# Combining the second FFN matrix's quarters ahead of time, and one difference of hidden tiles in the up stage

## Chip, cores and metric

The kernel runs on one core of a Trainium2 chip. The metric is the device time of one execution in microseconds.

## The reference, cut to what matters

A backbone of two layers over 1024 latent tokens and 256 context tokens of width 1024. Layer 0 mixes tokens by neighbourhood attention and differential attention (the "even attention"), layer 1 by grouped-query attention and a Hyena convolution. Each layer ends in a gated FFN with a hidden width of 2816:

```
def conv_ffn(h, w_up, conv_w, conv_b, w_down):
    g, v = jnp.split(h @ w_up, 2, axis=-1)
    g = dwconv3(g, conv_w, conv_b)
    return (jax.nn.silu(g) * v) @ w_down
```

Here `w_up` is 1024x5632 and `w_down` 2816x1024. Layer 1 needs no context tokens after its mixer.

## The kernel before, in words

Everything is kept transposed: 128 features on the partitions, tokens along the free axis. The hidden width is 22 tiles (`NJ`) of 128 features. Products in float32 are made of three matmuls (`mm3`, lines 73 to 75): both factors are split into a rounded high part and the rest, by a ScalarE copy (`split`, line 63) and a VectorE subtraction (line 68). A weight tile of 128x512 goes through `whalf`, a hidden tile through `hsplit`.

**Up stage** (`ffn`, lines 968 to 1018). For each hidden tile `j` the products are made with Strassen-like sums, the convolution and the gate run on ScalarE and VectorE, and the hidden tile `t` goes to DRAM (`hd[j]`, line 1018).

**Down stage** (`down`). The latent tokens' product with `w_down` is again Strassen-like: `w_down` is cut in four quarters (halves of the hidden width and of the output, called 11, 12, 21, 22), the hidden tiles as well (the hidden tiles' halves by the halves of the tokens), each of 11 tiles (`H`). There are four rounds `r`, each of 11 steps `k`. Rounds 0 to 2 have two products per step, into the PSUM sets `Y` and `Z` (24 matmuls of 128x512), round 3 one (12 matmuls). What a step needs is made beforehand:

- Weights, in `down_w` (lines 885 to 924): in round 0 four quarter tiles are loaded (256 KB each) and GpSimd makes three sums of them (lines 910 to 912); in round 1 two loads and one sum (917); in round 2 two loads; in round 3 two loads and one sum (923). `wnext` keeps 6 split halves ahead.
- Hidden tiles, in `prep` (1121 to 1137): in round 0 VectorE makes two differences (1126, 1127) and two splits; in rounds 1 and 2 GpSimd makes one difference (1131, 1135). Hidden tiles are loaded back from `hd` (1095) into tiles that the up stage has used.

In layer 0 the context tokens' down product (`down_ctx`) stands between the up stage and round 0.

**Even attention** (`attn_even`, lines 549 to 561). Four differential heads (`da_head`) and four pairs of neighbourhood heads (`na_pair`) take turns. Work goes in ticks (`tick`, line 507), nine for each of them: scores on TensorE into PSUM, VectorE takes them out (654), ScalarE makes exponents (631, 673), VectorE joins the two maps of a differential head (736), TensorE transposes (487) and multiplies (529, 755) one or two ticks later. GpSimd has little to do here: it normalizes the neighbourhood maps (635, 602) and makes a reciprocal root (134) for each group of a differential head, which VectorE needs next (152). Queries come by DMA into two pairs of buffers (462).

The order of instructions on each engine is set when the program is built, by a scheduler that works from its own estimate of the timing; an engine then runs its instructions in that order, and the DMA queue of SyncE issues its transfers in order too, each after what it waits for.

Of the kernel before, what the change touches and what calls it, by code (L numbers as in the profile page):

```python
# [2 lines left out]

# [1 line left out]

# [5 lines left out]
F32 = mybir.dt.float32  # L11
# [7 lines left out]
KT = 8  # L19
NL = 1024  # L20
# [19 lines left out]
class Kernel:  # L40
# [466 lines left out]
    def tick(self):  # L507

        self.step += 1
        due = [f for n, f in self.queue if n <= self.step]  # L510
        self.queue = [x for x in self.queue if x[0] > self.step]
        for f in due:
            f()
# [35 lines left out]
    def attn_even(self, first):  # L549

        with ExitStack() as es:
            p = self.pool(es, "ev", "right")
            pp = self.pool(es, "evp", psum=True)
            self.order(p, [("mn", 16, 6), ("sm", 16, 6), ("mc", 16, 6), ("s1", 16, 2), ("rsv", 16, 4), ("rsr", 16, 4), ("yeps", 16, 2),
                           ("ptc", 512, 2), ("y0", 256, 3), ("ysq", 256, 2), ("pt", 2048, 4), ("pr", NT, 6), ("tb", NAT, 2), ("v", NT, 2),
                           ("q", 512, 2), ("k", NT, 2)])
            n = {"D": 0, "N": 0}
            for c in "DNDNDNDN":
                (self.na_pair if c == "N" else self.da_head)(p, (self.ek, p)[sum(n.values()) % 2], pp, n[c], first if n == {"D": 0, "N": 0} else None)
                n[c] += 1  # L560
            self.flush()

    def load_v(self, p, src, c):

# [319 lines left out]

    def down_w(self, l, r, k, first=None):

        nc, W = self.nc, self.a["w_down"][l]
        op = nc.gpsimd.tensor_tensor
        A, S = ALU.add, ALU.subtract

        def get(names):

            src = [W[k + NJ // 2 * (n[1] == "2")][:, 512 * (n[0] == "2"):][:, :512] for n in names]
            if first:
                res = first
            elif k % 3 < 2 and r == 0 or r == 3 and (k % 2 == 1 or k > 9):
                res = [self.r2() for _ in names]
            else:
                res = []
                while len(res) < len(names):  # L900
                    t = self.wrp.tile([128, 1024], F32, tag="raw", name="raw", bufs=self.wr)
                    res += [t[:, :512], t[:, 512:]]
            for t, s in zip(res, src):
                self.wdma = nc.sync.dma_start(t, s).ins
            if first:
                self.wfirst = self.wdma
            return res
        if r == 0:
            a11, a21, a12, a22 = get(("11", "21", "12", "22"))
            op(a22, a21, a22, op=A)  # L910
            op(a11, a22, a11, op=S)
            op(a12, a12, a11, op=S)
            return [a11, a12] if first else [self.whalf(a11), self.whalf(a12)]
        if r == 1:
            a11, a21 = get(("11", "21"))
            z = self.whalf(a11)
            op(a21, a11, a21, op=S)
            return [self.whalf(a21), z]
        if r == 2:
            a12, a22 = get(("12", "22"))  # L920
            return [self.whalf(a22), self.whalf(a12)]
        a21, a22 = get(("21", "22"))
        op(a22, a21, a22, op=A)
        return [self.whalf(a22)]

    def ffn(self, l, hs, tv, xd, hd, sd, xp, last):

# [40 lines left out]
        for j in range(NJ):  # L968
            g = p.tile([128, nt], F32, tag="g", name="g", bufs=1)
            v = p.tile([128, NL], F32, tag="v", name="v", bufs=1)  # L970
            t = p.tile([128, nt], F32, tag="t", name="t", bufs=self.tb)
            late = (late + [t])[-2:]
            g1, g2, v1, v2 = (x[:, c:c + 512] for x in (g, v) for c in (0, 512))
            if ctx:
                c = self.bank("C")
            p1 = self.r2()
            if j < len(pre):
                X = None
                nc.sync.dma_start(p1, sd[j][:, :512])
# [24 lines left out]
            tt(v1, Y, p1, op=A)  # L1004
            if ctx:
                prod(c[:, NC:], "c2", True, w)
                prod(c[:, NC:], "c1", False)
            prod(Z, "22", False)
            tt(g2, u2, Z, op=A)
            if j == NJ - 1 and not ctx:  # L1010
                down = self.down(l, xd, hd, xp, last, late)
                next(down)
            self.conv(t, g, cw[:, j, :], spans)
            nc.scalar.activation(t[:, :nt], t[:, :nt], AF.Silu)
            tt(t[:, :NL], t[:, :NL], v, op=ALU.mult)
            if ctx:
                tt(t[:, NL:], t[:, NL:], c[:, NC:], op=ALU.mult)
            nc.sync.dma_start(hd[j][:, :nt], t[:, :nt])
# [5 lines left out]
    def down_ctx(self, xd, hd, xc, sq, bcx, yb, zb, last, late):  # L1024
# [2 lines left out]
        ps = [b.tile([128, 512], F32, tag="b", name="dn", bufs=4)[:, :NC] for b in (yb, zb) for _ in range(4)]  # L1027
        order = self.down_order()
        hid = {}
        first = [self.ff.tile([128, n], F32, tag=t, name="w0", bufs=1) for t, n in (("g", NT), ("v", NL))]  # L1030
        first = [t[:, c:c + 512] for t in first for c in (0, 512)]

        def prep(i):
            if i < NJ:
# [37 lines left out]
    def down(self, l, xd, hd, xp, last, late):  # L1072
# [10 lines left out]
        mid = [x for n in ("hi1", "lo1") for x in halves(self.act.tile([128, KT, 512], F32, tag=n, name="hid"), KT)]  # L1083
        tvs = [x for n in ("thi", "tlo") for x in halves(self.tp.tile([128, 4, 512], F32, tag=n, name="hid"), 4)]
        xs = [x for k in range(KT) for x in halves(xp.tile([128, 2, 512], F32, tag=f"x{k}", name="x"), 2)]
        B = {"22": tvs[0:4] + lat[0:7], "21": lat[7:16] + [mid[15], xs[15]], "12": xs[0:4] + mid[0:7], "11": tvs[4:8] + mid[7:14]}
        t12, p1, u3 = xs[4:8], mid[7:11], mid[11:15]
        self.xt = [[tvs[m], xs[8 + m]] for m in range(KT)]
        H = NJ // 2

        def load(b, k):
# [29 lines left out]
        def prep(r, k):  # L1121

            b11, b12, b21, b22 = (B[x][k] for x in ("11", "12", "21", "22"))
            if r == 0:
                z = hsplit(b22)
                tt(b12, b12, b11, op=S)
                tt(b22, b22, b12, op=S)
                return hsplit(b22), z
            if r == 1:
# [497 lines left out]
    def body(self):  # L1627
# [18 lines left out]
        self.actc = None  # L1646
        xd = dt((KT, 128, NT), "xd")
        self.nat = dt((8, 128, NAT), "nat")
        eac, ew = ExitStack(), ExitStack()
        with ExitStack() as es:  # L1650
            hs, mm = self.start(self.es, eac, ew, es)
# [226 lines left out]
```

## Time and profile before

| | |
|---|---|
| median of 3 runs | 3209.14 us (3207.26 to 3213.04) |
| the profiled execution | 3208.64 us, of which the span of the profile 3206.9 us |
| TensorE busy | 95% of the span |
| VectorE, ScalarE, GpSimd busy | 69%, 42%, 30% |
| DMA queue of SyncE | 434.35 MB, 41.4% of 16 engines |
| granted TensorE clock, mean | 0.984 |

The profile is of one execution. A busy share is an average over stages with different limits, so the stages are looked at one by one: the even attention from 521 to 885 us, the up stages from about 1040 to 1572 and 2540 to 2961 us, the down stages from 1644 to 1896 and from 2957 to 3202 us. A time in a row is counted from the start of the span.

### The profile page before, as it was taken

The page shows a single profiled execution, that of the slowest core. Times are in us where ns is not written, and L with a number is a line of the kernel's source. Part 1 is how long each engine was busy: PE and PEld are TensorE (multiplying, and loading weights), DVE is VectorE, ACT ScalarE, POOL GpSimd, SP SyncE. Part 2 cuts the span into 40 slices and gives each one's busy share as a digit, 9 for nine tenths or more (in the row PEclk, how much of TensorE's full clock was granted, in tenths as well). Part 3 has the DMA queues.
Part 4 walks back from the last instruction along what each step waited for, and adds up shares of the span by engine and source line. Part 5 has one row for each costly group of instructions (what it writes and reads, how often), then busy time and mean ns, then how long its engine had stood idle before and what let it go on. Part 6 is the DMA issues. An engine that isn't in the chain of part 4 may idle for free. (4 is left out here: it accounts for less than half of the span.)

```text
span 3206.9 us, 43513 instructions
## 1 busy us (share of the span) xinstructions
PE 3056.6 (95%) x15764; PEld 2458.4 (77%) x15764; DVE 2224.0 (69%) x3865; ACT 1340.9 (42%) x2374; POOL 964.0 (30%) x703
## 2 busy tenths in 40 slices
PE   7999989999999899999988989899999899999799
PEld 3567767777788788888876778787778677887677
DVE  7762454777757766766679687577665877766976
ACT  4322213777735333333434452226663533433343
POOL 5530220222202422222135344012330443323662
PEclk9999999999999999999999999999999999999899
DMA  6798884443253322111584446222104332224644
GB/s 239 224 301 269 246 261 129 122 126 106 81 168 111 102 82 73 65 73 65 174 288 154 135 161 163 94 76 59 36 27 148 122 109 89 86 92 154 223 144 149
DMA packets 269815, 443.03 MB, mean 138 GB/s; under 512 B 27936, under 2 KB 160160, under 8 KB 262944
## 3 DMA queue, kind: packets, MB, share of 16 engines
q1 hardware_dynamic: 265280, 434.35, 41.4%
q10 hardware_dynamic: 4320, 5.90, 0.5%
q8 instruction: 124, 2.03, 0.3%
q14 instruction: 91, 0.75, 0.1%
HBM read 338.31 MB, written 101.84 MB: 137 GB/s over the span
## 5 line engine op out<-in xcount | busy, mean ns | idle before, releaser
L68 DVE TENSOR_TENSOR wlo<-raw,whi 128x512 fp32r<-128x512 f32 x456 | 351.6, 783 | 194.4 <-ACT whi L63 187.8
L63 ACT CAST whi<-raw 128x512 fp32r<-128x512 f32 x456 | 275.3, 619 | 458.6 <-PE u L74 75.3
L134 POOL TENSOR_TENSOR rsr<-rsv,misc 128x8 f32<-128x8 f32 (+3 forms) x87 | 114.1, 1313 | 591.1 <-DVE rsv L131 343.6
L857 POOL TENSOR_TENSOR S<-raw 128x512 f32<-128x512 f32 x88 | 142.7, 1622 | 482.9 <-DMA raw<-in_w_up 407.0
L476 PE MATMUL S<-k,q 128*128 128x512 f32 (+2 forms) x1088 | 262.4, 365 | 6.4 <-DMA q<-qs 3.0
L74 PE MATMUL dn<-hs,whi 128*128 128x512 f32 x616 | 244.2, 400 | 16.5 <-DVE hs L68 16.5
L73 PE MATMUL mm<-whi,hi 128*128 128x512 f32 (+1 forms) x624 | 241.9, 389 | 2.1 <-ACT vst L393 1.1
L73 PE MATMUL dn<-hs,whi 128*128 128x512 f32 x616 | 217.5, 405 | 26.1 <-ACT hs L63 18.8
L74 PE MATMUL mm<-wlo,hi 128*128 128x512 f32 (+1 forms) x624 | 237.2, 380 | 1.6 <-DVE wlo L68 1.6
L75 PE MATMUL dn<-hs,wlo 128*128 128x512 f32 x616 | 234.9, 396 | 3.2 <-DVE wlo L68 3.2
L75 PE MATMUL mm<-whi,lo 128*128 128x512 f32 (+1 forms) x624 | 237.1, 381 | 0.7 <-DVE lo L252 0.7
L824 DVE SCALAR_TENSOR_TENSOR t<-g,cw,t 128x1008 f32<-128x1008 f32 (+1 forms) x220 | 206.3, 970 | 44.2 <-ACT t L822 43.9
L476 PEld LDWEIGHTS S<-k,q 128*128 128x128 f32 x1088 | 167.0, 189 | 42.3 <-DVE mn L654 13.0
L487 PE MATMUL T<-ident,pr 128*128 128x128 f32 x1312 | 190.5, 276 | 6.1 <-DVE pr L736 2.3
L654 DVE CUSTOM_DVE_ANT_0 pr<-S,misc,mn 128x512 f32<-128x512 f32 x256 | 185.3, 745 | 6.1 <-PE S L476 4.4
L68 DVE TENSOR_TENSOR wlo<-S,whi 128x512 fp32r<-128x512 f32 x176 | 158.1, 916 | 42.7 <-ACT whi L63 42.6
L673 ACT ACTIVATE pr<-pr,mn 128x1280 f32<-128x1280 f32 x128 | 174.5, 1367 | 30.6 <-DVE mn L654 23.1
L487 PEld LDWEIGHTS T<-ident,pr 128*128 128x128 f32 x1312 | 151.7, 141 | 44.0 <-issue 25.4
L490 ACT COPY pt<-T 128x512 f32<-128x512 f32 (+1 forms) x256 | 131.4, 523 | 85.3 <-PE T L487 82.5
L73 PEld LDWEIGHTS dn<-hs,whi 128*128 128x128 f32 x616 | 118.4, 194 | 59.3 <-ACT hs L63 23.0
L68 DVE TENSOR_TENSOR hs<-hid,hs 128x512 fp32r<-128x512 f32 x142 | 137.1, 974 | 37.7 <-ACT hs L63 36.0
L74 PEld LDWEIGHTS dn<-hs,whi 128*128 128x128 f32 x616 | 118.5, 193 | 48.4 <-DVE hs L68 23.9
(359 smaller groups left out, 7981.6 us busy)
## 6 DMA issues: line engine op xcount, KB each, us to landing
adaw<-in_w_ada SPq DMA_DIRECT2D x48, 1024.0 KB, 6.8
raw<-in_w_up SPq DMA_DIRECT2D x88, 512.0 KB, 4.0
raw<-in_w_down SPq DMA_DIRECT2D x132, 256.0 KB, 3.1
r<-in_w_down SPq DMA_DIRECT2D x84, 256.0 KB, 5.4
q<-qs SPq DMA_DIRECT2D x160, 128.0 KB, 2.2
hid<-hd SPq DMA_DIRECT2D x78, 256.0 KB, 5.3
qs<-qsg SPq DMA_DIRECT2D x120, 128.0 KB, 3.9
hd<-t SPq DMA_DIRECT2D x22, 640.0 KB, 2.9
```

The costliest lines, as they stand in the source:

```text
L63: nc.scalar.copy(hi, src)
L68: nc.vector.tensor_tensor(lo, src, f32(hi), op=ALU.subtract)
L73: mm(ps, lhsT=lh, rhs=rh, start=first, stop=False, skip_group_check=more)
L74: mm(ps, lhsT=lh, rhs=rl, start=False, stop=False, skip_group_check=more)
L75: mm(ps, lhsT=ll, rhs=rh, start=False, stop=last, skip_group_check=more)
L476: self.nc.tensor.matmul(ps, lhsT=q[:, s, c:c + 128], rhs=k[:, k0:k0 + n], start=s == 0, stop=s == 1)
L487: nc.tensor.transpose(tp[:, s, :], p_[:, k * 128:(k + 1) * 128], self.ident)
L490: eng(pt[:, s0:s0 + sn, col:col + 128], tp[:, :sn])
L654: self.nc.vector.tensor_tensor_reduce(out=dst, in0=s, in1=bias, scale=1.0, scalar=init, op0=ALU.add, op1=ALU.min, accum_out=mn)
L673: nc.scalar.activation(pr, pr, AF.Exp, bias=m[:, 1:2], scale=-1.0, accum_out=sums[j])
L824: nc.vector.scalar_tensor_tensor(t[:, o:o + n], g[:, i:i + n], cw[:, w:w + 1], t[:, o:o + n], op0=ALU.mult, op1=ALU.add)
L857: nc.gpsimd.tensor_tensor(got[n], x, y, op=op)
```

## The change

A GpSimd job is added to the even attention (`wd_steps`): for each layer and each `k` it loads the four quarter tiles of `w_down` in three column pieces (192, 192 and 128 columns, so 66 pieces in all), makes four sums of them in place and stores all four in a new DRAM tensor `ws`. Two buffers of 768 columns hold the pieces. `tick` takes two steps of this job each time (one load, one set of sums with its store). `down_w` then loads ready sums: two quarter tiles in round 0, two in rounds 1 and 2, one in round 3, and GpSimd makes no sum there. The first 11 hidden tiles have their first token half subtracted from the second in the up stage, before they are stored, so that one of the two differences of round 0 falls away. Some buffers of hidden tiles trade places.

```diff
@@ tick
         self.step += 1
+        self.beside(2)
@@ attn_even
+            self.bg = chain(self.wd_steps(0, p), self.wd_steps(1, p))
...
             self.flush()
+            self.beside(100)
@@ down_w
-        if r == 0:
-            a11, a21, a12, a22 = get(("11", "21", "12", "22"))
-            op(a22, a21, a22, op=A)
-            op(a11, a22, a11, op=S)
-            op(a12, a12, a11, op=S)
-            return [a11, a12] if first else [self.whalf(a11), self.whalf(a12)]
-        if r == 1:
-            a11, a21 = get(("11", "21"))
-            z = self.whalf(a11)
-            op(a21, a11, a21, op=S)
-            return [self.whalf(a21), z]
-        if r == 2:
-            a12, a22 = get(("12", "22"))
-            return [self.whalf(a22), self.whalf(a12)]
-        a21, a22 = get(("21", "22"))
-        op(a22, a21, a22, op=A)
-        return [self.whalf(a22)]
+        x = get((("S2", "S4"), ("11", "S3"), ("22", "12"), ("S1",))[r])
+        if first:
+            return x[:2]
+        w = [self.whalf(t) for t in x[:1 + (r < 3)]]
+        return w[::-1] if r == 1 else w
+    def wd_steps(self, l, p):
+        nc, W = self.nc, self.a["w_down"][l]
+        op = nc.gpsimd.tensor_tensor
+        A, S = ALU.add, ALU.subtract
+        for k in range(NJ // 2):
+            for c, n in ((0, 192), (192, 192), (384, 128)):
+                t = p.tile([128, 4, 192], F32, tag="wd", name="wd", bufs=2)[:, :, :n]
+                for i in range(2):
+                    nc.sync.dma_start(t[:, 2 * i:2 * i + 2], W[k + NJ // 2 * i].rearrange("p (h c) -> p h c", h=2)[:, :, c:c + n])
+                yield
+                a11, a21, a12, a22 = (t[:, i] for i in range(4))
+                op(a22, a21, a22, op=A)
+                op(a21, a11, a21, op=S)
+                op(a11, a22, a11, op=S)
+                op(a12, a12, a11, op=S)
+                nc.sync.dma_start(self.ws[l][k][:, :, c:c + n], t)
+                yield
@@ ffn, before the hidden tile is stored
+            if j < NJ // 2:
+                tt(t[:, 512:NL], t[:, 512:NL], t[:, :512], op=ALU.subtract)
@@ down, prep, round 0
                 z = hsplit(b22)
-                tt(b12, b12, b11, op=S)
                 tt(b22, b22, b12, op=S)
```

**Order on GpSimd, even attention.** Lines of the changed kernel are shifted: 134 is 135 there, 635 is 639, 602 is 606, 1131 is 1149, 857 is 861. Before, from the end of a pair of neighbourhood heads into the next differential head, GpSimd has:

```order
L602 TENSOR_SCALAR pr<-pr,sm 128x256 x4
L635 TENSOR_SCALAR pr<-pr,sm 128x640 x6
L635 TENSOR_SCALAR pr<-pr,sm 128x512 x2
L134 TENSOR_TENSOR rsr<-rsv,misc 128x2 x3
L635 TENSOR_SCALAR pr<-pr,sm 128x512 x2
```

In the change, inside a differential head (`wd` is the piece being summed):

```order
L926 TENSOR_TENSOR wd<-wd 128x192
L927 TENSOR_TENSOR wd<-wd 128x192
L135 TENSOR_TENSOR rsr<-rsv,misc 128x2
L928 TENSOR_TENSOR wd<-wd 128x192
L929 TENSOR_TENSOR wd<-wd 128x192
L926 TENSOR_TENSOR wd<-wd 128x192
L927 TENSOR_TENSOR wd<-wd 128x192
L928 TENSOR_TENSOR wd<-wd 128x192
L929 TENSOR_TENSOR wd<-wd 128x192
L135 TENSOR_TENSOR rsr<-rsv,misc 128x2
```

The reciprocal roots `rsr` that followed each other directly now stand behind or among sums of a piece.

**Order on SyncE's queue, even attention.** Before, queries follow queries (here with a head's values `v`):

```order
L462 DMA q_5060<-qs0_80 128x256 x2
L462 DMA q_5063<-qs0_80 128x256 x2
L462 DMA q_5286<-qs1_81 128x256 x2
L462 DMA q_5289<-qs1_81 128x256 x2
L462 DMA q_5173<-qs1_81 128x256 x2
```

In the change, a store of a piece (`ws0<-wd`) and the load of a later one into the same buffer stand between them:

```order
L923 DMA wd_6183<-in_w_down 128x2x192 x2
L930 DMA ws0_88<-wd_6120 512x1x128
L463 DMA q_6415<-qs0_80 128x256 x2
L570 DMA v_6536<-vsb_85 128x10x128
L923 DMA wd_6257<-in_w_down 128x2x192 x2
L930 DMA ws0_88<-wd_6183 512x1x192
L463 DMA q_6670<-qs1_81 128x256 x2
L923 DMA wd_6315<-in_w_down 128x2x128 x2
```

So a query's load is issued only after a store whose sums are done, and after a load whose buffer is free.

**Order on GpSimd, start of layer 1's down stage.** Before, behind the last sums of the up stage (`S`), triples of line 910 to 912 follow, 11 in all; the first of those shown:

```order
L910 TENSOR_TENSOR r<-r 128x512
L911 TENSOR_TENSOR r<-r 128x512
L912 TENSOR_TENSOR r<-r 128x512
L910 TENSOR_TENSOR r<-r 128x512
L911 TENSOR_TENSOR r<-r 128x512
L912 TENSOR_TENSOR r<-r 128x512
```

In the change the next after the up stage's sums is round 1's difference of hidden tiles:

```order
L861 TENSOR_TENSOR S<-raw,S 128x512
L1149 TENSOR_TENSOR hid<-hid 128x512 x2
L1149 TENSOR_TENSOR hid<-x,hid 128x512 x2
L1149 TENSOR_TENSOR hid<-hid 128x512 x7
```

In round 0 GpSimd has nothing left.

## Rows read from the trace of the kernel before

**Rows 1.** The page's first part: busy time of each engine, its share of the span, and its instructions.

```profile
PE 3056.6 (95%) x15764; PEld 2458.4 (77%) x15764; DVE 2224.0 (69%) x3865; ACT 1340.9 (42%) x2374; POOL 964.0 (30%) x703
```

**Rows 2.** Six stretches of the run, in us from the span's start: the whole even attention, one differential head, one pair of neighbourhood heads, the up stage of layer 0, the up stage of layer 1, and the start of layer 1's down stage. The columns are the stretch's length, the busy time of each engine with its instructions in brackets, the granted TensorE clock as a share of full speed, the mean busy share of the 16 DMA engines, and GB/s.

```profile
521.00:885.00 364.00, 352.79 (x2218) 284.92 (x2217) 284.69 (x964) 262.22 (x567) 71.73 (x100) 1.00 0.36 109
625.00:675.00 50.00, 48.11 (x284) 42.05 (x284) 42.63 (x137) 37.40 (x79) 7.42 (x10) 1.00 0.35 106
675.00:712.00 37.00, 36.70 (x254) 27.03 (x254) 26.25 (x99) 25.41 (x59) 10.19 (x15) 1.00 0.43 129
1100.00:1500.00 400.00, 400.00 (x2119) 345.42 (x2118) 275.69 (x350) 139.62 (x211) 100.51 (x64) 1.00 0.20 73
2720.00:2920.00 200.00, 200.00 (x884) 165.62 (x883) 141.92 (x188) 77.74 (x120) 59.26 (x40) 1.00 0.24 86
2960.00:3000.00 40.00, 21.09 (x64) 15.30 (x63) 37.73 (x29) 10.47 (x17) 33.41 (x21) 0.70 0.94 332
```

**Rows 3.** The same view, for the instructions alone that write or read the down stage's PSUM tiles `dn`: the four rounds of layer 0, then the four of layer 1. A round has 264 matmuls, the last 132; some counts are a few over, since a stretch's edge can cut a neighbour.

```profile
1644.00:1726.00 82.00, 68.20 (x264) 50.87 (x264) 1.70 (x5) 2.12 (x4) 0.94 0.71 237
1726.00:1792.00 66.00, 62.45 (x263) 49.81 (x264) 2.99 (x5) 1.12 (x3) 0.97 0.39 128
1792.00:1858.00 66.00, 61.89 (x267) 49.23 (x265) 4.82 (x8) 1.12 (x2) 1.00 0.44 141
1858.00:1896.00 38.00, 32.40 (x132) 25.61 (x132) 3.14 (x6) 0.00 (x0) 0.96 0.53 172
2957.00:3047.00 90.00, 67.36 (x264) 53.01 (x265) 0.00 (x0) 2.16 (x4) 0.87 0.70 240
3047.00:3109.00 62.00, 60.61 (x267) 49.53 (x266) 3.45 (x6) 1.63 (x3) 1.00 0.47 160
3109.00:3172.00 63.00, 60.83 (x265) 49.06 (x264) 2.80 (x5) 0.68 (x2) 1.00 0.45 146
3172.00:3202.00 30.00, 30.00 (x134) 24.75 (x132) 8.75 (x13) 0.00 (x0) 1.00 0.31 117
```

**Rows 4.** Waits of TensorE in the first round of layer 1: who waited for whom, us in total, times, longest.

```profile
PE dn L73 <- ACT hs L63: 13.7, 3, 8.7
PE dn L74 <- DVE hs L68: 6.2, 3, 3.0
```

**Rows 5.** VectorE in order of time at the start of that round (start, duration, line, operation; a bracket would give the idle time before it).

```profile
...
2970.25 1.75 DVE L68 TENSOR_TENSOR hs<-hid,hs 128x512 fp32r<-128x512 f32 x1
2971.92 2.27 DVE L824 SCALAR_TENSOR_TENSOR t<-g,cw,t 128x1008 f32<-128x1008 f32 x1
...
2988.82 2.29 DVE L1015 TENSOR_TENSOR t<-t,v 128x1024 f32<-128x1024 f32 x1
```

**Rows 6.** ScalarE in order of time there; the bracket is its idle time before, and what ended it.

```profile
...
2986.10 1.06 ACT L1014 ACTIVATE t<-t 128x1024 f32<-128x1024 f32 x1 [14.01 <-DVE t L824]
2987.06 0.60 ACT L63 CAST hs<-hid 128x512 fp32r<-128x512 f32 x1
```

**Rows 7.** Instructions of one line or tile: durations in ns as least/median/most, then the first and last start. Two of VectorE in the down stage, both inputs in SBUF; one of VectorE in the up stage, one input in PSUM; one of GpSimd in the down stage, and two of GpSimd elsewhere, for their sizes.

```profile
L68 DVE TENSOR_TENSOR hs<-hid,hs x142: 674/685/1784, 1577.5 to 3189.4; 128x512 fp32r<-128x512 f32 x142
L1126 DVE TENSOR_TENSOR hid<-hid x14: 679/1655/1787, 1645.7 to 3024.5; 128x512 f32<-128x512 f32 x14
L992 DVE TENSOR_TENSOR r<-Y,r x44: 675/681/692, 1063.1 to 2944.3; 128x512 f32<-128x512 f32 x44
L911 POOL TENSOR_TENSOR r<-r x15: 1588/1622/2122, 1645.8 to 3003.3; 128x512 f32<-128x512 f32 x15
L360 POOL TENSOR_TENSOR qz<-qy,gqack x8: 458/478/975, 1909.1 to 1939.1; 128x128 f32<-128x128 f32 x8
L857 POOL TENSOR_TENSOR S<-raw x88: 1281/1307/6639, 1023.1 to 2925.3; 128x512 f32<-128x512 f32 x88
```

**Rows 8.** VectorE in the even attention, its groups of instructions: line, operation, out<-in, shapes, count | busy us, mean ns of one | idle time before.

```profile
L654 DVE CUSTOM_DVE_ANT_0 pr<-S,misc,mn 128x512 f32<-128x512 f32 x128 | 92.4, 744 | 3.3 <-PE S L476 2.3
L736 DVE SCALAR_TENSOR_TENSOR pr<-pr,sm 128x1280 f32<-128x1280 f32 (+1 forms) x40 | 53.3, 1332 | 0.2
L152 DVE TENSOR_TENSOR dg<-ident,rsr 128x256 f32<-128x256 f32 x20 | 8.4, 421 | 3.7 <-POOL rsr L134 3.7
```

**Rows 9.** Waits in the even attention, of the DMA queue of SyncE and of VectorE: us in total, times, longest.

```profile
SPq L462 <- PE S L476: 148.8, 40, 9.8
DVE dg L152 <- POOL rsr L134: 3.7, 7, 0.6
```

**Rows 10.** DMA issues: out<-in, engine, operation, count, KB each, median us from issue to landing.

```profile
r<-in_w_down SPq DMA_DIRECT2D x84, 256.0 KB, 5.4
xd<-x SPq DMA_DIRECT2D x40, 256.0 KB, 2.3
raw<-in_w_up SPq DMA_DIRECT2D x18, 256.0 KB, 2.6
natab<-in_na_tab SPq DMA_DIRECT2D x8, 448.0 KB, 4.9
nat<-natab SPq DMA_DIRECT2D x8, 448.0 KB, 3.3
```

**Rows 11.** SyncE's queue in order of time: the same load of two successive periods (a differential head and a pair of neighbourhood heads), two periods apart.

```profile
623.28 0.37 SPq L566 DMA_DIRECT2D v<-vsa  x1
...
802.62 0.37 SPq L566 DMA_DIRECT2D v<-vsa  x1
```

More of the change, by code (lines that the diff above doesn't have):

```diff
@@ L2 @@
 from contextlib import ExitStack, nullcontext
+from itertools import chain
 import numpy as np
@@ L554, in attn_even @@
             self.order(p, [("mn", 16, 6), ("sm", 16, 6), ("mc", 16, 6), ("s1", 16, 2), ("rsv", 16, 4), ("rsr", 16, 4), ("yeps", 16, 2),
-                           ("ptc", 512, 2), ("y0", 256, 3), ("ysq", 256, 2), ("pt", 2048, 4), ("pr", NT, 6), ("tb", NAT, 2), ("v", NT, 2),
+                           ("ptc", 512, 2), ("y0", 256, 3), ("ysq", 256, 2), ("pt", 2048, 4), ("pr", NT, 6), ("tb", NAT, 2), ("v", NT, 2), ("wd", 768, 2),
                            ("q", 512, 2), ("k", NT, 2)])
+            self.bg = chain(self.wd_steps(0, p), self.wd_steps(1, p))
             n = {"D": 0, "N": 0}
@@ L885, in down_w @@
     def down_w(self, l, r, k, first=None):
-        nc, W = self.nc, self.a["w_down"][l]
-        op = nc.gpsimd.tensor_tensor
-        A, S = ALU.add, ALU.subtract
+        nc, W, ws = self.nc, self.a["w_down"][l], self.ws[l]
         def get(names):
-            src = [W[k + NJ // 2 * (n[1] == "2")][:, 512 * (n[0] == "2"):][:, :512] for n in names]
+            src = [ws[k][:, "S2 S3 S4 S1".split().index(n)] if n[0] == "S" else W[k + NJ // 2 * (n[1] == "2")][:, 512 * (n[0] == "2"):][:, :512] for n in names]
             if first:
@@ L898, in get @@
             else:
[L899 to L902, printed above, removed]
+                t = self.wrp.tile([128, 1024], F32, tag="raw", name="raw", bufs=self.wr)
+                res = [t[:, :512], t[:, 512:]]
             for t, s in zip(res, src):
@@ L907, in get, with beside @@
             return res
-        if r == 0:
-            a11, a21, a12, a22 = get(("11", "21", "12", "22"))
-            op(a22, a21, a22, op=A)
-            op(a11, a22, a11, op=S)
-            op(a12, a12, a11, op=S)
-            return [a11, a12] if first else [self.whalf(a11), self.whalf(a12)]
-        if r == 1:
-            a11, a21 = get(("11", "21"))
-            z = self.whalf(a11)
-            op(a21, a11, a21, op=S)
-            return [self.whalf(a21), z]
-        if r == 2:
-            a12, a22 = get(("12", "22"))
-            return [self.whalf(a22), self.whalf(a12)]
-        a21, a22 = get(("21", "22"))
-        op(a22, a21, a22, op=A)
-        return [self.whalf(a22)]
+        x = get((("S2", "S4"), ("11", "S3"), ("22", "12"), ("S1",))[r])
[20 more added lines that the diff above has]
+                yield
+    def beside(self, n):
+        while n and self.bg:
+            n -= 1
+            if next(self.bg, 1):
+                self.bg = None
+    bg = None
     def ffn(self, l, hs, tv, xd, hd, sd, xp, last):
@@ L1029, in down_ctx @@
         hid = {}
-        first = [self.ff.tile([128, n], F32, tag=t, name="w0", bufs=1) for t, n in (("g", NT), ("v", NL))]
-        first = [t[:, c:c + 512] for t in first for c in (0, 512)]
+        first = self.ff.tile([128, NT], F32, tag="g", name="w0", bufs=1)
+        first = [first[:, c:c + 512] for c in (0, 512)]
         def prep(i):
@@ L1085, in down @@
         xs = [x for k in range(KT) for x in halves(xp.tile([128, 2, 512], F32, tag=f"x{k}", name="x"), 2)]
-        B = {"22": tvs[0:4] + lat[0:7], "21": lat[7:16] + [mid[15], xs[15]], "12": xs[0:4] + mid[0:7], "11": tvs[4:8] + mid[7:14]}
+        B = {"22": tvs[0:2] + xs[1::-1] + lat[0:7], "21": lat[7:16] + [mid[15], xs[15]], "12": tvs[3:1:-1] + xs[2:4] + mid[0:7], "11": tvs[4:8] + mid[7:14]}
         t12, p1, u3 = xs[4:8], mid[7:11], mid[11:15]
-        self.xt = [[tvs[m], xs[8 + m]] for m in range(KT)]
+        self.xt = [[xs[3 - m] if m in (2, 3) else tvs[m], xs[8 + m]] for m in range(KT)]
         H = NJ // 2
@@ L1648, in body @@
         self.nat = dt((8, 128, NAT), "nat")
+        self.ws = [dt((NJ // 2, 128, 4, 512), f"ws{l}") for l in range(2)]
         eac, ew = ExitStack(), ExitStack()
```

## The prediction

> **What bounds the kernel now.** I read the page first: TensorE is busy 95% of the span [rows 1], so time can come only from stretches where it idles or is throttled, or be lost where it now runs. The table of stretches comes next [rows 2]. In both up stages TensorE has no idle time (400 us of 400, 200 of 200), and 884 matmuls of 128x512 in 200 us put one at 0.226 us. Then the down stages, by round [rows 3]: a round of 264 matmuls needs 264 x 0.226 = 59.7 us, the last of 132 needs 29.9. Against that the eight stretches last 82, 66, 66 and 38 us in layer 0, and 90, 62, 63 and 30 in layer 1. Lost are 22.3, 6.3, 6.3 and 8.1, then 30.3, 2.3, 3.3 and 0.1 us: 79 us, of which 52.6 in the two rounds 0. This includes the throttle: the clock of rounds 0 is 0.94 and 0.87 on average, 1.00 in most others, so parts of them ran at 1.2 instead of 2.4 GHz, after idling.
>
> Why does round 0 idle? At the start of layer 1's, TensorE waits for the hidden tiles' splits, 13.7 us for the ScalarE half and 6.2 for the VectorE half [rows 4]. In that stretch VectorE is busy 37.7 us of 40, GpSimd 33.4, and the DMA engines 94% at 332 GB/s [rows 2]. VectorE's work isn't much, it is slow: a split of 128x512 takes 0.685 us in the middle of the distribution and up to 1.78, and the difference of line 1126 has 1.655 as its median [rows 7]. The timeline shows 1.75 us for a split and 2.27 and 2.29 for the convolution and gate of the last up tile [rows 5]. ScalarE is kept in its order by that: it waits 14.0 us for the convolution (824) before its activation, and only then makes the split that TensorE wants [rows 6]. An operation of VectorE with one input in PSUM stays at 0.68 to 0.69 us in all 44 cases of the up stage, where GpSimd sums as well [rows 7]. So it is VectorE operations with both inputs in SBUF that wait for a running sum of GpSimd, by up to 1.78 - 0.68 = 1.1 us each.
>
> **Down stage: the gain.** Round 0 loses all three sums of GpSimd per step, half of the weight loads (512 KB instead of 1 MB) and one of the two differences on VectorE. Per step two weight tiles and three hidden tiles of 256 KB remain instead of four and three, 1.31 MB instead of 1.84 MB. At 24 x 0.226 = 5.4 us a step that is 243 GB/s, where the full engines gave 332 [rows 2]: not a bound any more, whereas 1.84 MB need 5.5 us, which was one. VectorE has two weight splits, two hidden splits and one difference, 5 x 0.68 = 3.4 us of 5.4, with no GpSimd operation to wait for. What is left is close to what round 1 has today (a little GpSimd work, loads at 39 to 47% of the engines), and that loses 6.3 and 2.3 us [rows 3]. Layer 0 keeps besides the entry from the context part; I put its round 0 at 9 us lost instead of 22.3. In layer 1 the stretch holds 14 matmuls of the up stage too (278 in all, 3.2 us), and VectorE has the last tile's convolution and gate to make before it can catch up, some 5 us; I put it at 10 lost instead of 30.3. Bounds: nothing gained, and 6.3 and 5.5 lost (round 1's loss, with the 3.2). Gain 13.3 + 20.3 = 33.6, between 0 and 41.
>
> Rounds 1 and 3 lose one GpSimd sum a step and round 3 half of its loads; of the 26 us lost in the six later rounds I take 5 back, between 0 and 10, since GpSimd's difference of hidden tiles stays and the waits at the rounds' ends are for PSUM and for the next norm. Gain of the down stages: 39 us.
>
> **Up stage: nothing.** 22 differences of 0.68 us (up to 1.78) go to VectorE, which is busy 276 of 400 us in layer 0 and 142 of 200 in layer 1 while TensorE has no idle time [rows 2]. The cover is the tile buffers: the gate isn't on TensorE's way until the down stage, and the last tile has no such difference. If the cover were gone it would be 22 x 1.1 = 24 us.
>
> **Even attention: the cost.** 66 pieces come in, each with two loads, four sums and a store.
>
> GpSimd: a sum of 128 columns takes 0.46 us at least, of 512 columns 1.28 [rows 7]; by a straight line 192 columns take 0.60 (an estimate). A `k` takes 8 x 0.60 + 4 x 0.46 = 6.6 us, 22 of them 146 us. A period of two heads is 18 ticks and lasts (802.62 - 623.28)/2 = 89.7 us [rows 11], 4.98 us a tick, so 66 ticks are 329 us, in which GpSimd would be busy 45% with sums, beside the 72 us of 364 that it has [rows 2]. There is room.
>
> DMA: 22 x 2.1 MB (read and written) = 46 MB in 329 us, 140 GB/s on top of 109 GB/s at a share of 0.36 [rows 2]; at the same share per byte the engines reach 0.82. Room again.
>
> VectorE: the bulk of its work there, line 654, reads scores from PSUM [rows 8], a form that rows 7 show free of waits. The 40 joins of line 736 and the 20 of line 152 have both inputs in SBUF. With GpSimd at a sum 45% of the time and half of 0.60 us left on average, each waits 0.13 us: 8 us. The 20 reciprocal roots (134) stand behind or among the sums, and VectorE waits for each root already in 7 cases, 3.7 us [rows 9]; one sum ahead makes 20 x 0.6 = 12 us. All 60 lie in differential heads, where VectorE is busy 42.6 of 50 us [rows 2], so most of it shows: 15 of the 20 us. Bounds: 0, if VectorE's idle time takes it all, and the two rivals below.
>
> SyncE's queue: a buffer's turn is load, sums, store. A load of 256 KB lands in 2.6 us, a store in 2.3 [rows 10]; with the second issue of the load, 2.2 us of sums on average, a store of up to 384 KB at some 2.6 and the hand-overs it is 8.2 us, 4.1 per piece with two buffers. That is under the 4.98 of a tick. **The Trainium skill**, "SBUF — State Buffer", section "The DMA setup-cost knee", states about 2 us fixed plus the bytes at 436 GB/s. For a piece that makes 2.9 us each way, an estimate, and about the same turn; rows 10 show 5.4 us for 256 KB in the crowded down stage, which that formula doesn't cover, so the measured rows go into the rival. Queries' loads wait in this queue anyway, 148.8 us in 40 waits for their buffers [rows 9], and with two pairs of buffers a load is issued about two ticks before its use, so a few us behind a store cost nothing as long as the chain keeps pace.
>
> **Sum.** The profiled execution took 3208.6 us. Minus 39, plus 15: 3184.6. The median of the runs is 0.5 above the profiled one, so **3185 us**.
>
> **Rivals.**
>
> *The attention hides it all.* VectorE idles 7.4 us per differential head and TensorE's waits there are short, so the 15 us may vanish, and round 0 may come down to round 1's loss with up to 5 us more. For it: the rows of the PSUM form. Against it: the differential heads' VectorE at 85%. Time 3209 - 44 = 3165 us, chance 0.26.
>
> *Only half of the gain.* If round 0 was held by the loads and the last tile's convolution rather than by GpSimd, its loss falls by half, 17 us, with 3 elsewhere. For it: the DMA engines at 94%; against it: they lose 29% of the bytes as well. Time 3209 - 20 + 15 = 3204 us, chance 0.11.
>
> *The pieces set the pace.* SyncE's queue is in order: a piece's load waits for the store two pieces back, and queries wait behind. The nearest chain of this kind under load is the mask tables': 4.9 us to load 448 KB, 3.3 to store [rows 10]. With sums of 1.62/1.28 their length [rows 7], 2.8 us, 0.4 for the second issue and 0.3 for hand-overs, a turn is 11.7 us, 5.85 per piece: 66 x (5.85 - 4.98) = 57 us, less the two ticks of slack, 10. With the 15 on VectorE it comes to 3209 - 39 + 62 = 3232 us, slower. It decides from (39 - 15 + 10)/66 = 0.5 us over the tick, a piece in 5.5 us. Chance 0.10.
>
> *VectorE pays in full in the differential heads.* Each of the 60 operations waits a whole sum of its size, 1.1 x 0.60/1.28 = 0.52 us, 31 us, and each reciprocal root half a piece, 1.2 us x 20 = 24. Time 3209 - 39 + 55 = 3225 us, chance 0.07. This is what the Trainium skill's "SBUF — State Buffer", section "Who interferes with whom", allows at worst: an exclusive lock, where a VectorE instruction with two SBUF inputs and a GpSimd operation block each other for the whole instruction. By that rule, rows 5 and 7 agree on the lock; how often the two meet it doesn't say.
>
> That the change doesn't do what it says is not a rival: the order shows no sum of GpSimd left in round 0.
>
> **How the numbers follow.** My forecast has 0.46. A measurement of this kernel can tell about 0.2%, 6.4 us, so "faster" ends at 3202.7 and "slower" begins at 3215.6. Faster: 0.46 + 0.26 and a part of the half-gain case, 0.73. Same: 0.10. Slower: the last two, 0.17. The range takes in the first rival with some of its bounds (3209 - 51 = 3158) and the half gain, and reaches to 3218, short of the two slow cases: 3158 to 3218.
>
> **What would show it.** In the profile after: GpSimd with no operation in rounds 0 and VectorE's splits there at 0.68 us; `dn` stretches of round 0 near 69 and 70 us instead of 82 and 90; the period of two heads at 89.7 + 4 us (15 us over four periods); operations of line 736's form longer than now; the chain of a piece at or under 5 us, and TensorE's waits for queries as short as before. Wrong would be: TensorE waiting for queries in the attention by tens of us (the pieces' pace), a period of over 100 us, or round 0 still losing 20 us with VectorE at 0.68 (then the loads held it).

## The result, and the profile after

The changed kernel takes 3242.0 us (median of 7 runs, 3226.6 to 3243.8) where the kernel before took 3209.6 beside it: a ratio of 1.0081, 95% interval 1.0065 to 1.0097. It is slower by 0.8%; 3185 was forecast, with 3158 to 3218 as range. The profiled execution has a span of 3242.0 us. Medians here and below are of undisturbed runs; one run of the experiment e6_store_pool took 6377.6 us and is left out.

Stretches of the kernel after, in the columns of [rows 2]: the even attention, one differential head, one pair of neighbourhood heads, the start of layer 1's down stage.

```profile
521.00:972.00 451.00, 377.55 (x2217) 305.45 (x2215) 295.97 (x968) 264.45 (x567) 231.49 (x364) 0.91 0.65 194
644.00:709.00 65.00, 51.29 (x259) 43.66 (x259) 40.92 (x121) 33.57 (x72) 36.58 (x54) 0.84 0.65 193
714.00:756.00 42.00, 35.23 (x228) 24.62 (x228) 24.48 (x92) 23.35 (x51) 22.96 (x39) 0.96 0.71 215
...
3021.00:3061.00 40.00, 35.74 (x146) 27.91 (x146) 29.54 (x46) 19.27 (x32) 0.00 (x0) 0.96 0.88 318
```

Its down stage in the view of [rows 3]: round 0 of layer 0, rounds 0 and 1 of layer 1.

```profile
1726.90:1790.30 63.40, 62.23 (x264) 50.42 (x265) 1.97 (x4) 2.18 (x4) 0.97 0.60 211
3011.20:3084.40 73.20, 63.08 (x264) 49.98 (x264) 1.25 (x2) 2.31 (x4) 0.98 0.70 244
3084.60:3144.30 59.70, 59.70 (x265) 49.44 (x264) 2.02 (x4) 1.47 (x3) 1.00 0.41 137
```

GpSimd makes no sum of weights in rounds 0 any more, as forecast, and VectorE's splits of hidden tiles there take 0.69 us, where the prediction said 0.68. Their least/median/most in ns, before (layer 0, layer 1) and after:

```profile
L68 DVE TENSOR_TENSOR hs<-hid,hs x19: 677/962/1782, 1653.6 to 1722.3; 128x512 fp32r<-128x512 f32 x19
L68 DVE TENSOR_TENSOR hs<-hid,hs x24: 678/860/1781, 2970.2 to 3043.8; 128x512 fp32r<-128x512 f32 x24
L69 DVE TENSOR_TENSOR hs<-hid,hs x15: 683/692/695, 1745.1 to 1786.3; 128x512 fp32r<-128x512 f32 x15
L69 DVE TENSOR_TENSOR hs<-hid,hs x21: 684/686/693, 3010.7 to 3080.4; 128x512 fp32r<-128x512 f32 x21
```

The down stages became 51.5 us shorter: measured from a round's first matmul to the next round's first, the lost time of all eight rounds falls from 77.9 to 26.3 us. The even attention became 87 us longer, 451 instead of 364. Together that is +35.5, and the span grew by 35.1: the rest of the kernel cancels out, with 4 us less between the attention and layer 0's down stage and 4 more between the two down stages. Within the attention TensorE's idle time went from 11.2 to 73.5 us (+62), and the same 2217 matmuls took 24.8 us more at a granted clock of 0.91 instead of 1.00: more of them ran at 1.2 instead of 2.4 GHz, after the idling.

Waits of that stretch after; the row of SyncE's queue for the queries and that of the roots answer to [rows 9].

```profile
POOL wd L926 <- DMA wd<-in_w_down: 217.2, 51, 59.1
...
PE S L477 <- DMA q<-qs: 49.2, 13, 10.4
...
DVE dg L153 <- POOL rsr L135: 40.0, 15, 8.8
```

The same view for SyncE's queue:

```profile
SPq L923 <- DMA ws<-wd: 79.5, 49, 4.1
SPq L930 <- POOL wd L929: 39.3, 27, 5.0
SPq L463 <- PE S L477: 27.9, 21, 4.8
```

Before, the queue stood 148.8 us with a query's load in hand whose buffer was not free: it was early. Now that is 27.9 us; it stands before pieces' loads and stores instead, and TensorE waits for queries. GpSimd stands before sums whose load has not landed (one of 59.1 us at the entry aside), and the roots behind them come late. Its order of time shows one such turn (start, duration, then in the bracket the idle time before):

```profile
678.86 0.59 POOL L926 TENSOR_TENSOR wd<-wd 128x192 f32<-128x192 f32 x1 [4.21 <-DMA wd<-in_w_down]
679.53 0.59 POOL L927 TENSOR_TENSOR wd<-wd 128x192 f32<-128x192 f32 x1
680.07 0.71 POOL L135 TENSOR_TENSOR rsr<-rsv,misc 128x2 f32<-128x2 f32 x1
```

And two periods, as in [rows 11], last (871.65 - 642.75)/2 = 114.5 us each instead of 89.7. So two of the prediction's signs of being wrong came: TensorE waits for queries by tens of us, and a period takes over 100.

```profile
642.75 0.38 SPq L570 DMA_DIRECT2D v<-vsa  x1
...
871.65 0.38 SPq L570 DMA_DIRECT2D v<-vsa  x1
```

### The profile page after: what moved, and what is told of

Read it like the earlier page. It is cut to its first block, busy times and chain, and to the rows that moved or that the text cites. A ratio compares the mean times of both kernels' runs of the same rounds, so it can differ in the third digit from the quotient of the medians.

```text
span 3242.0 us, 43905 instructions
## 1 busy us (share of the span) xinstructions
PE 3064.0 (95%) x15764; PEld 2475.1 (76%) x15764; DVE 2139.3 (66%) x3865; ACT 1346.1 (42%) x2374; POOL 941.9 (29%) x857
## 4 chain that ended last, share of the span: by engine, by line
PE 59%; DVE 6%; DMA 5%; issue 2%; ACT 1%; POOL 1%; SPq 1%; DVEq 0%; ACTq 0%; POOLq 0%
PE dn L74 4%; PE dn L75 4%; PE dn L76 4%; PE Y L74 3%; PE Y L75 3%; PE O L531 3%; PE Y L76 3%; PE S L477 3%; PE T L488 3%; PE mm L74 2%; PE mm L76 2%; PE mm L75 2%; PE Z L74 2%; PE Z L75 2%; PE Z L76 2%; PE X L74 2%
## 5 line engine op out<-in xcount | busy, mean ns | idle before, releaser
L69 DVE TENSOR_TENSOR wlo<-raw,whi 128x512 fp32r<-128x512 f32 x456 | 328.1, 732 | 242.3 <-ACT whi L64 231.3
L477 PE MATMUL S<-k,q 128*128 128x512 f32 (+2 forms) x1088 | 271.2, 376 | 67.7 <-DMA q<-qs 49.2
L477 PEld LDWEIGHTS S<-k,q 128*128 128x128 f32 x1088 | 175.8, 199 | 103.0 <-DVE mn L658 18.6
L75 PE MATMUL dn<-hs,whi 128*128 128x512 f32 x616 | 240.9, 393 | 3.5 <-DVE hs L69 3.5
L74 PE MATMUL dn<-hs,whi 128*128 128x512 f32 x616 | 208.4, 394 | 9.7 <-ACT hs L64 5.0
L74 PEld LDWEIGHTS mm<-whi,hi 128*128 128x128 f32 x624 | 119.9, 192 | 47.5 <-issue 13.7
L74 PE MATMUL Y<-t34h,whi 128*128 128x512 f32 x352 | 139.3, 396 | 8.9 <-DVE r L1011 5.6
L64 ACT CAST whi<-S 128x512 fp32r<-128x512 f32 x176 | 102.7, 618 | 101.0 <-POOL S L861 84.2
```

Source lines behind the costliest of these rows:

```text
L64: nc.scalar.copy(hi, src)
L69: nc.vector.tensor_tensor(lo, src, f32(hi), op=ALU.subtract)
L74: mm(ps, lhsT=lh, rhs=rh, start=first, stop=False, skip_group_check=more)
L75: mm(ps, lhsT=lh, rhs=rl, start=False, stop=False, skip_group_check=more)
L477: self.nc.tensor.matmul(ps, lhsT=q[:, s, c:c + 128], rhs=k[:, k0:k0 + n], start=s == 0, stop=s == 1)
```

## Experiments

In the table, "even" is the time from the first scores to the last product of the even attention, "GQA" the first to the last scores of the grouped-query attention, in the profiled execution; "ratio" is to the kernel before in the same session.

| kernel | pieces | even | GQA | median us | ratio (95%) |
|---|---|---|---|---|---|
| before | 0 | 364 | 220 | 3209.6 | 1 |
| after | 66 | 451 | 220 | 3242.0 | 1.0081 (1.0065, 1.0097) |
| e1_no_job | 0 | 369 | 219 | 3166.1 | 0.9857 (0.9840, 0.9873) |
| e2_job_only | 66 | 446 | 219 | 3296.9 | 1.0266 (1.0245, 1.0287) |
| e3_no_sums | 66, no sums | 437 | 219 | 3232.8 | 1.0065 (1.0045, 1.0085) |
| e4_no_dma | 66, sums alone | 399 | 219 | 3200.0 | 0.9974 (0.9956, 0.9992) |
| e6_store_pool | 66 | 432 | 220 | 3236.9 | 1.0082 (1.0063, 1.0100) |
| e10_thirds | 88 smaller | 442 | 220 | 3235.9 | 1.0086 (1.0064, 1.0107) |
| e8_half | 33 | 403 | 220 | 3225.6 | 1.0054 (1.0035, 1.0072) |
| e7_split | 33 + 33 in GQA | 402 | 240 | 3218.4 | 1.0029 (1.0015, 1.0042) |
| e11_paced | 33, held | 384 | 219 | 3191.8 | 0.9938 (0.9922, 0.9954) |
| e12_split_paced | 33 + 33, held | 384 | 219 | **3170.8** | 0.9871 (0.9854, 0.9889) |
| e13_all_paced | 66, held | 428 | 220 | 3232.1 | 1.0060 (1.0043, 1.0077) |
| e14_loads_held | 33 + 33, loads held | 377 | 239 | 3184.7 | 0.9914 (0.9896, 0.9933) |

**Gain and cost apart.** e1_no_job makes no pieces; its down stage loads plain quarter tiles in the place of the ready sums, as many and as large. e2_job_only has the pieces and the down stage of before.

```diff
-            self.bg = chain(self.wd_steps(0, p), self.wd_steps(1, p))
```

> The changed kernel without the job in the even attention. Round 0, 1 and 3 of the down stage load plain quarter tiles of the same size in place of the sums, so the weights are not the right ones; every load, split and product of the down stage is as in the change. All theories: the even attention is back at 364 us, the down stages keep the gain of the change (lost time 26 us instead of 78), so the time is 3209 - 51 = 3158 us. If it is above 3175, the gain depends on something else than the sums that are gone.

> The kernel before with the job added to the even attention and its result not used. All theories: the even attention takes 451 us instead of 364, the rest is as before: 3209 + 87 = 3296 us. If the two parts don't add up (e1 and e2 together against the change), the change's order of instructions elsewhere has a share.

Without the pieces it is 3166.1 us, 45 under the 3211.0 beside it, and the down stages lose 25.5 us; the pieces alone cost 86 (two runs). So the gain is the down stage's and the cost is the pieces'. The two add up to 41 us, though, where the change cost 32, and e1 is 8 us over what was expected, 5 of them in the attention. Both differences come mostly from the stretch between the two down stages: it takes 1061 us before, 1065 after, 1069 in e1 and 1070 in e2, and from 1061 to 1080 in the kernels here that have no pieces in it. No cause of this was looked for. So a difference of less than 20 us between the times of two kernels says little about the attention, and the lengths of the stages carry the argument.

**What of a piece costs?** e3_no_sums leaves the four sums out and stores the quarters as loaded; e4_no_dma loads two tiles once, sums them over and over and stores nothing (its down stage is that of e1).

```diff
-                op(a22, a21, a22, op=A)
-                op(a21, a11, a21, op=S)
-                op(a11, a22, a11, op=S)
-                op(a12, a12, a11, op=S)
```

> The changed kernel with the four sums of each piece left out: pieces are loaded and stored again, the weights in the down stage are plain quarters. Theory A (a piece's turn load, sums, store through two buffers, in SyncE's order, sets the pace, now 6.2 us a piece): a turn loses about 2.5 us of 12.4, a piece then comes each 5.0 us, about the tick; the attention lasts 375 to 395 us and queries are still waited for now and then: 3170 to 3190 us. Theory B (GpSimd's order: the reciprocal roots stand behind sums that wait for their loads) and theory C (the lock between sums and VectorE): nothing is left to wait for on GpSimd, the attention is back at 364 to 370 us: 3158 to 3165 us.

> The changed kernel with the four sums of every piece made in the even attention on two tiles that are loaded once; no piece is loaded or stored after that, and the down stage loads plain quarters as in e1. Theory A and B: with no transfer to wait for, the attention is back at 364 to 372 us: 3158 to 3166 us. Theory C (the lock): VectorE waits for the sums as before, the attention stays at 400 us or more: 3195 us or more.

Every theory missed e3: without a sum there are still 68 of the 82 us (437 against 369). The roots are on time there, the queries are not (from 521 to 905 us):

```profile
PE S L477 <- DMA q<-qs: 64.6, 14, 11.8
...
DVE dg L153 <- POOL rsr L135: 1.6, 4, 0.6
```

e4 costs 30 us: theories A and B, at 364 to 372 us, missed it, and C, at 400 or more, is near. Its 66 pieces were through by 740 us, 3.2 us each, though a piece is asked for once a tick of 4.98, and the 30 us are lost by then: the first join of its third differential head comes at 741.3 us, in e1 at 710.7. The joins of VectorE have a mean of 1920 ns instead of the 1332 of [rows 8], but the excess isn't spread over them: three take 16.47, 5.96 and 4.49 us, the other 37 have a mean of 1348 ns. TensorE waits 22.9 us for them in three waits. Here are all joins, the longest, and the last of the 31 sums that run beside it without a gap:

```profile
L741 DVE SCALAR_TENSOR_TENSOR pr<-pr,sm 128x1280 f32<-128x1280 f32 (+1 forms) x40 | 76.8, 1920 | 0.2
539.03 16.47 DVE L741 SCALAR_TENSOR_TENSOR pr<-pr,sm 128x1280 f32<-128x1280 f32 x1
553.56 0.58 POOL L931 TENSOR_TENSOR wd<-wd 128x192 f32<-128x192 f32 x1
```

The join ends 1.4 us after GpSimd's row of sums does: it didn't wait for the running sum alone, the next ones passed it too. In the change no join takes over 2.0 us, so this price isn't a part of the 82.

**SyncE's order, or the transfers themselves?** Four kernels of one session: stores issued by GpSimd behind their sums (e6); three buffers of 128 columns, each load written ahead of the sums before it (e10); layer 0's pieces alone, one step a tick, with layer 1's down stage making its sums as before (e8); and layer 0's so, with layer 1's in the grouped-query attention, two steps a tick (e7).

```diff
e6
-                nc.sync.dma_start(self.ws[l][k][:, :, c:c + n], t)
+                nc.gpsimd.dma_start(self.ws[l][k][:, :, c:c + n], t)
e8 and e7
-        self.beside(2)
+        self.beside(1)
-            self.bg = chain(self.wd_steps(0, p), self.wd_steps(1, p))
+            self.bg = self.wd_steps(0, p)
```

> The pieces' stores are issued by GpSimd, right behind the sums that they store; the loads stay in SyncE's queue. Theory 'order' (a store waits in SyncE's in-order queue for its sums, which wait for their load: load issue 1.1 + landing 3.2 + four sums 2.4 + store issue 0.6 = 7.3 us in a row where a tick has 4.98, and the queries stand behind it): SyncE now waits only until the buffer's old store has landed; a buffer's round trip is 1.1 + 3.2 + 2.4 + 0.6 + 3.4 = 10.7 us for two pieces, 5.35 us a piece, still a little over a tick. The even attention falls from 451 us to 380 to 405, the time to 3185 to 3205. Theory 'transfers' (87 MB at 194 GB/s beside the attention make every landing late): nothing changes, 3235 to 3245. Theory 'GpSimd' (roots late behind sums that wait for a load): GpSimd gets 66 issues more, 3240 to 3260.

> Same sums, same bytes, same queue; but pieces of 128 columns in three buffers of the same total size, and a piece's load is issued before the sums and the store of the piece ahead of it. Theory 'order': a load has landed when its sums come, a store waits only for sums that are running; a buffer's round trip of some 1.1 + 2.9 + 1.9 + 0.6 + 3 = 9.5 us serves three pieces, 3.2 us a piece where 3.7 is the pace asked for. Attention 365 to 390 us instead of 451, time 3165 to 3190, faster than both kernels. Theory 'transfers': the bytes are the same and the rows shorter (512 bytes), so 3235 or more. Theory 'GpSimd' only in its part that waits for loads: the roots come earlier too, 3200 to 3225 if the running sums alone delay them.

> Only layer 0's 33 pieces, at half the pace (one step a tick: the load in one tick, sums and store in the next); layer 1's down stage makes its sums itself, as the kernel before does. Theory 'order': no load waits for a store and no store for a load; attention 370 to 380 us. Layer 1's first round loses about 30 us again instead of 13: 3166 (no pieces at all) + 17 + 0 to 10 = 3180 to 3195. Theory 'transfers': half the bytes cost half of what all cost, 3166 + 17 + 40 = 3215 to 3230.

> All 66 pieces, but layer 0's in the even attention at half the pace and layer 1's in the grouped-query attention, one piece a tick of some 12 us (with five row buffers there instead of six, for room). Theory 'order': the even attention is 370 to 380 us, the grouped-query attention 0 to 10 us longer, the down stages as with the whole change: 3166 + 4 + 0 to 15 = 3168 to 3190, faster than both kernels. Theory 'transfers': the bytes are all there, and cost about what they did, 3215 to 3245.

The theory "order" missed all four, and "transfers" named all four times; e6's attention did get 19 us shorter, though, and its time hides that behind 12 us more between the down stages. But e8's trace showed that a premise of both was false. Its 33 pieces should have filled the stage; they ran from 532 to 743 us (first sums), 6.6 us each, as fast as two buffers let them. The order is fixed when the program is built, and a piece was put wherever its buffer was expected to be free; the ticks hold nothing back. So e8 holds its own comparison, 155 us with pieces and 155 us without:

```profile
602.00:757.00 155.00, 134.19 (x807) 105.37 (x807) 99.90 (x344) 94.12 (x205) 79.86 (x128) 0.92 0.66 198
759.00:914.00 155.00, 152.04 (x960) 125.52 (x959) 122.27 (x414) 113.77 (x253) 32.25 (x46) 1.00 0.31 94
```

With pieces TensorE gets 807 matmuls done in the time of 960. The two stretches don't begin at the same place of a period; cut at the first joins of the differential heads (641.1, 748.2 and 838.0 us), a period takes 107.1 us with pieces and 89.8 without. What TensorE and VectorE stood for in the first stretch:

```profile
POOL wd L948 <- DMA wd<-in_w_down: 39.1, 15, 7.8
...
DVE dg L153 <- POOL rsr L135: 14.0, 5, 4.5
PE S L477 <- DMA q<-qs: 12.1, 4, 5.6
PEld T L488 <- POOL rsr L135: 7.0, 2, 4.9
```

**Pieces held to their tick.** In e11 (otherwise e8), e12 (e7) and e13 (the whole change) a load stands in SyncE's order behind the last query load written before it (`ql`), and the sums in GpSimd's behind the last root or scaling (`pl`).

```diff
+                with self.behind(self.ql):
                     nc.sync.dma_start(t[:, 2 * i:2 * i + 2], W[k ...
+                with self.behind(self.pl):
                     op(a22, a21, a22, op=A)
```

> As the kernel with layer 0's 33 pieces alone, which ran them between 532 and 743 us, 6.4 us a piece (the compiler's order lets a piece go as soon as its buffers are free, whatever the tick), with one thing changed: a piece's load stands in SyncE's order behind the queries of its tick, and its sums in GpSimd's behind the last root or scaling before them, so that the pieces spread over the whole stage, one in some 10 us. Theory 'queues' (what costs is GpSimd and SyncE standing in order before a load or a store that has not landed: there 39 us on loads, 14 on late roots, 17 on late queries between 602 and 757): nothing of a piece is waited for at this pace, attention 403 -> 370 to 382 us, time 3195 to 3207. Theory 'transfers' (each piece costs about 1.1 us by its bytes and sums, wherever it stands): attention 395 to 405, time 3218 to 3230.

> All 66 pieces, layer 0's in the even attention and layer 1's in the grouped-query attention as in the split kernel (3218 us, even attention 402 us, grouped-query attention 240 instead of 219), and now held behind the queries and the roots or scalings of their tick. Theory 'queues': even attention 370 to 382, grouped-query attention 222 to 232, time 3175 to 3195, faster than both kernels. Theory 'transfers': 3212 to 3225, as without the holding.

> The whole change, all 66 pieces in the even attention, with the same holding behind the tick's queries and roots. Theory 'queues': 66 round trips of 10.7 us through two buffers need 353 us of an attention that has 369, so SyncE still stands before stores, but GpSimd no longer before loads ahead of roots: attention 451 -> 395 to 430 us, time 3190 to 3222. Theory 'transfers': 3232 to 3245, no change.

With the same bytes and sums as e8 and e7, the times fall from 3225.6 to 3191.8 and from 3218.4 to 3170.8 us: 3 and 4 us better than "queues" had said, and 26 and 41 outside of "transfers" (the attention, 384 us, is 2 over the range of "queues" in both). e11's pieces spread from 530 to 873 us, and the stretches of e8's comparison are alike now, 915 and 919 matmuls:

```profile
602.00:757.00 155.00, 146.57 (x915) 117.96 (x914) 122.37 (x411) 108.95 (x229) 60.22 (x101) 0.99 0.58 174
759.00:914.00 155.00, 145.54 (x919) 116.59 (x917) 108.06 (x361) 103.72 (x231) 57.26 (x92) 0.99 0.48 145
```

Over the whole stage it is the roots that come on time now: VectorE's waits for them fall from 23.8 us in e8 to 3.2 in e11. TensorE's waits for queries stay, 17.6 and 18.5 us against 9.7 in e1. Of the cost 15 us are left; whether these waits are their cause was not tried.

In the grouped-query attention the same 33 pieces cost 21 us free and nothing held. There the transposes wait for the scaling of the probabilities (line 1622 in e7, 1625 in e12, 1624 in e14), which stands behind the sums. Free (e7):

```profile
POOL wd L926 <- DMA wd<-in_w_down: 105.0, 21, 24.5
...
PEld T L488 <- POOL pr L1622: 25.5, 22, 3.1
PE T L488 <- POOL pr L1622: 15.9, 16, 2.6
```

Held (e12), where TensorE's waits for scalings are down to 0.9 and 1.7 us:

```profile
POOL pr L1625 <- DVE sm L1623: 76.9, 19, 31.8
...
POOL wd L928 <- DMA wd<-in_w_down: 9.3, 4, 4.0
```

With 135 GB/s there against 132 in e7, it is not the transfers. e13 keeps its attention in the range of "queues" (428 us), but its time, 3232, is where "transfers" had it. All 66 pieces take the stage at their own pace, from 526 to 934 us, which leaves the holding nothing to spread; that this is the reason was not tried further.

**Which order matters where?** e14 is e12 without the holding of the sums.

> The split kernel with half of the holding: the loads stand behind their tick's queries in SyncE's order, but the sums are free in GpSimd's. Theory 'SyncE' (late queries behind pieces are what costs): as with both held, 3168 to 3180, grouped-query attention 219 to 223 us. Theory 'GpSimd' (the roots and scalings stand behind sums that wait for their load; in the split kernel's grouped-query attention the transposes waited 41 us for scalings, GpSimd 105 us for loads, and with both held neither did): most of the cost comes back, grouped-query attention 230 to 242 us, even attention 390 to 403, time 3195 to 3218.

Each theory is right in one stage, and the time, 3184.7, lies between their ranges. In the even attention holding the loads is enough (377 us; the wait for roots falls from 21.1 us in e7 to 7.0). It is even 7 us shorter than with the sums held too, and TensorE waits 8.2 us for queries instead of e12's 17.4; loads alone held here and both in the next stage was not tried. In the grouped-query attention the whole cost is back, 239 us, and the wait with it:

```profile
POOL wd L927 <- DMA wd<-in_w_down: 105.0, 24, 24.4
...
PEld T L488 <- POOL pr L1624: 21.7, 19, 3.8
PE T L488 <- POOL pr L1624: 14.1, 10, 3.3
```

e12, 3170.8 us (3170.3 to 3173.2), beats both kernels: 1.3% under before and, by the two ratios, 2.1% under after, and within 5 us of e1, which makes no pieces at all.

## Why the prediction was wrong

**The step that failed is SyncE's queue**, "4.1 per piece with two buffers. That is under the 4.98 of a tick", and the conclusion that late stores cost nothing "as long as the chain keeps pace". The turn was mis-sized: 66 pieces went from 524 to 934 us, 6.2 us each. A store waits in the queue for its sums and these for their load, so load and store of successive pieces hardly overlap, and under this traffic a load of 192 KB lands in 3.2 us and a store of 384 KB in 3.4. The worse fault was the premise behind it, that a tick paces the pieces. e8 and e4 show that it doesn't: the order of each queue is fixed ahead, by estimates. The orders ahead of the prediction had pieces' stores and loads before the queries, and sums before the roots; they were priced as a few us and as one sum, not as a wait for whatever the piece itself waits for.

**The rival "the pieces set the pace"** gave 3232 us, near the 3242, from 5.85 us a piece. Its place is the right one and its rule is not, so that it came so near is partly luck: it charges only what a piece takes beyond a tick. e3's pieces took 4.85 us (524 to 844), under the tick, and cost 68; e8's 33 pieces, with twice the ticks they need, cost 34. What is shown is that a piece costs 0.6 to 1.2 us where it stands in the queues ahead of work that is due (21 us for 33 in GQA in e7, 82 for 66 in the change), and less where it doesn't (15 us for 33 pieces in e11, 8 for as many in e14, none in GQA in e12). How the 82 us (451 against e1's 369; 5 of the 87 are there without any piece) split between late queries and late roots isn't settled: e3, without sums, has 68 of them, but its queries are later than the change's (64.9 us of waits against 49.2).

**VectorE**: 8 us were put on joins and diagonals; they became (1397 - 1332) x 40 + (553 - 421) x 20 ns = 5.2 us longer, near enough. The roots, at 12 us, were mis-sized: VectorE waited 40.0 us for them instead of 3.7, since not one sum stood ahead of a root but a sum that waited for its load. "VectorE pays in full" didn't come about at this pace, and its worst, one whole sum of 0.52 us for each operation, isn't the worst: in e4, where sums run without a break, one join took 16.47 us.

**Down stage**: the mechanism was right as far as VectorE's splits show it (0.69 us now); no run takes the GpSimd sums away and leaves the bytes of their loads. The size was low, 51.5 us instead of 39. Layer 0's round 0 lost 3.8 (9 forecast), layer 1's 13.6 (10). The rest is the six later rounds, 5 forecast and 25.7 - 8.9 = 16.8 measured; rounds 1 lose 0.04 us each now. I had taken their loss for one at the rounds' ends; what removed it was not tried. Of layer 1's round 0, the difference made in the up stage is worth 7 to 9 us (e8 and e11, which keep the old sums there, lose 21.2 and 23.0), the ready sums the other 8 to 9.

**Up stage**, nothing forecast: from the first to the last product into `Y` layer 0 took 518.5 instead of 517.3 us, layer 1 408.8 instead of 404.7. In the kernels with the same up stage layer 1's is between 405 and 415, so up to some us of it may be the change's.

**The chances**: "Room again" for the DMA and "There is room" for GpSimd were true as shares (0.65 and 51%) and said nothing about order. I counted room, and the 0.73 for faster stood on that.

## What to carry to other kernels

Background work on in-order queues is paid less in busy time than in what stands behind its waits: for each queue that it joins, ask what is next in line when its load has not landed. Don't take the place in the source for a pace: read the order of each queue, and tie background transfers behind the foreground's own, and background operations behind the operation that others wait for. Compare a stretch with and without such work inside one run, as e8 allowed, to see its cost and who waits; then move the same work to another place in the order, as e11 did, to tell order from bytes.

## What the runs showed of the hardware

Transfers beside compute can cost nothing: the grouped-query attention ran with 33 pieces (11 x 2.1 = 23 MB), 135 GB/s at a DMA share of 0.46, in 219 us as without them (e12, e1). The Trainium skill says so too ("SBUF — State Buffer", section "Who interferes with whom": DMA never contends with a compute engine); these rows agree.

A VectorE operation with both inputs in SBUF can be passed by many GpSimd sums, not only by the one that runs: in e4 a join, 1.5 us long elsewhere, took 16.47 us beside 31 sums in a row, and two others 5.96 and 4.49.

GpSimd passes nothing ahead of an operation that waits for a transfer: in e7 its scalings stood behind sums that waited 105 us. The Trainium skill states it ("Perfetto Trace Analysis", section "Tensor Engine Instruction (MATMUL, LD_WEIGHTS)": ScalarE, VectorE and GpSimd are strictly first in, first out), and the trace agrees.

Idling is paid twice: of the attention's 87 us, 25 are matmuls at the lower clock, where TensorE's waits for queries reach 10.4 us. In e8's first stretch the clock was 0.92, in its second, without pieces, 1.00.
